# A streaming-encoder block on one core: two thirds of the depthwise taps moved from VectorE to ScalarE and GpSimd, and a fifth pair by seven products in four column groups

## The chip, the core and the metric

The kernel runs on one core of one Trainium2 chip. The metric is the device time of one execution in microseconds. Before the change it is 2029.14 us, the median of three runs (2028.86 to 2029.4). The profile is of one more execution, which took 2028.23 us.

In the profile PE is TensorE's matmuls, PEld its weight loads, DVE is VectorE, ACT is ScalarE, POOL is GpSimd and SP is SyncE, whose queue issues most DMAs.

## The reference

One layer over 256 rows of width 4096, all in float32. The part that the change touches is the first half: a norm, a wide input product, attention on 16 heads of 128, and beside it a convolution module whose depthwise part has 31 taps over 2048 channels.

```python
xn = rms_norm(h, norm_in_g[i])
proj = xn @ w_in[i]                       # 4096 x 14336
q, k, v, z_a, a_c, g_c, z_c = jnp.split(proj, ...)
y_a = chunked_attention(q, k, v, rel_table[i])
...
u = a * jax.nn.sigmoid(g)                 # conv_module
u = jnp.pad(u, ((0, 0), (CONV_K - 1, 0), (0, 0)))
u = depthwise(u, w_dw) + b_dw             # 31 causal taps for each of 2048 channels
u = jax.nn.silu(layer_norm(u, ln_g, ln_b))
y_c = u @ w_pw + b_pw
...
h = h + jnp.concatenate([y_a, y_c], axis=-1) @ w_out[i]
gate = jax.nn.sigmoid(rms_norm(h, ple_norm_g[i]) @ w_ple_gate[i] + b_ple_gate[i])
h = h + gate * (p[i] @ w_ple[i])
```

## The kernel before

**Products.** Every large product is made in float32 precision from parts that TensorE takes at its fast rate. A weight tile `wt` (128 x 1024: two column groups of 512) comes by DMA; ScalarE casts its high part `wh` (L204) and VectorE subtracts to get the low part `wl` (L205, `parts_of`). Each block product is then three matmuls of 128 x 512: high by high, low by high, high by low. Three tiles each of `wh` and `wl` rotate, and five of `wt`.

**Pairs by seven products.** `mixed_product` (L342) makes two column groups at once. It goes over 16 pairs of 128-row blocks, in an order that a text table gives. A plain pair takes eight block products, 24 matmuls. A pair marked `*` or `+` takes seven, 21 matmuls (Strassen's way): VectorE adds up the needed sums of weight blocks (`ua`, `ub`, L467 to L475) and each of the two sum tiles is cast and subtracted in turn (`uh`, `ul`). For a `+` the first sums come from the DMA: SP's queue loads a tile and GpSimd's queue adds a second transfer on top of it (L421), issued up to three pairs ahead by `sums_ahead`. The sums on the side of the activations (`combinations`) are made once and kept.

**Stages.** `scaled_pair` (L524) makes one such product from the input weights and scales it on the way out; its last four instructions on VectorE are L538. The program calls it in this order: convolution group 0, convolution group 1, (q0, k0), (v0, v1), attention 0, convolution group 2, (q1, k1), attention 1, convolution group 3, (q2, k2), (q3, v2), attention 2, layer norm, (k3, v3). The groups use the tables `early` (four pairs by seven), `early_five` (five) or `early_six` (six).

**Taps.** After a convolution group, `glu_conv` (L736) transposes the gated result to channels by time (`uT`, four blocks of 128 channels by 256) and puts 4 x 31 small jobs into the list `later`. Each is one instruction on VectorE, `conv_tap` (L718): `cv = uT * tap + cv` over 226 to 256 elements, both tensors in SBUF. `fill(n)` takes the next n jobs from `later`; `mixed_product` calls it after each pair with a number from a table (`early_fills`, `six_fills`), so the taps of one group run among the weight subtractions of the next ones:

```python
early_fills = (5, 6, 1, 5, 6, 1, 5, 6, 1, 5, 6, 1, 2, 5, 5, 4)
for i in range(4):
    for k in reversed(range(TAPS)):
        later.append(partial(conv_tap, cv, uT, i, 4 * c + i, k))
```

Each engine runs its instructions in the order of the program as the scheduler wrote it, so an instruction that waits holds up everything behind it on its engine. GpSimd before the change has little to do: the accumulating DMAs (L421), four memsets of the attention bias (L943) and a handful of tiny powers (L139).

Of the kernel before, what the change touches and what calls it, by code (L numbers as in the profile page):

```python
# [25 lines left out]
def hybrid_block(  # L26
# [23 lines left out]
    nc = tc.nc  # L50
    _, T, D = x.shape
# [5 lines left out]
    TAPS = w_dw.shape[1]  # L57
    PAD = TAPS - 1
# [23 lines left out]
    spool = pool("spool", 2, first_scratch, 1)  # L82
# [11 lines left out]
    o_q, o_k, o_v, o_za = 0, AW, 2 * AW, 3 * AW  # L94
# [117 lines left out]
    recent = []  # L212

    @contextmanager
    def queued_behind(made):

        with ExitStack() as queued:
            for ins in made:
                queued.enter_context(tc.issue_after(ins.ins))
            yield  # L220
# [112 lines left out]
    early_six = units("1 3 5 0+ 7 2* 9 4+ 11 6* 13 8+ 15 10* 12 14")  # L333

    early_fills = (5, 6, 1, 5, 6, 1, 5, 6, 1, 5, 6, 1, 2, 5, 5, 4)
    six_fills = (6, 6, 1, 5, 1, 5, 1, 5, 1, 5, 1, 5, 1, 6, 7, 7)
    norm = units("1 3 5 7 9 11 0+ 13 2* 15 4+ 8 6* 10 12 14")
    norm_fills = (7, 8, 8, 8, 6, 4, 2, 3, 2, 3, 2, 2, 0, 6, 5, 5)
# [379 lines left out]
    def conv_tap(cv, uT, i, b, k):  # L718
# [4 lines left out]
        else:  # L723
# [2 lines left out]
                cv[:, i, PAD - k :], ALU.mult, ALU.add,  # L726
            )

    def more_combinations(pair):

        if pair in (7, 9):
            c = (pair + 1) // 2
            xS[2 * c] = act.tile([P, 2, 2, T], F32R, tag="act", name="comb_x"), 0
            later.extendleft(reversed(combinations(c)))

    def glu_conv(c):  # L736
        if c == 0:
            sg, gate = scaled_pair(
                w_in0, o_a, o_g - o_a, first, r_x, (1,), begin=first_pairs
            )  # L740
        else:
            sg, gate = scaled_pair(
                w_in0, o_a + c * NB, o_g - o_a,
                *((early, r_x, early_fills) if c == 1 else (early_six, r_x, six_fills)),
                ahead=more_combinations if c == 2 else None,
            )
        for h in range(NH):
            nc.scalar.activation(gate[:, h, :], gate[:, h, :], AF.Sigmoid)
            tt(sg[:, h, :], sg[:, h, :], gate[:, h, :], ALU.mult)
        uT = spool.tile([P, 4, T], F32, tag="hd", name="uT", bufs=5)  # L750
        for pair in range(2):
            pt = tmp_psum()
            for i in range(2):
                for h in range(NH):
                    b = 2 * pair + i
                    nc.tensor.transpose(
                        pt[:, i * T + h * P : i * T + (h + 1) * P],
                        sg[:, h, b * P : (b + 1) * P],
                        ident,
                    )  # L760
            nc.scalar.copy(
                uT[:, 2 * pair : 2 * pair + 2, :], pt.rearrange("q (i t) -> q i t", t=T)
            )
        cv = act.tile([P, 4, T], F32, tag="act", name="cv")
        for i in range(4):
            for k in reversed(range(TAPS)):
                later.append(partial(conv_tap, cv, uT, i, 4 * c + i, k))
        conv.append(cv)


# [116 lines left out]
    def attention(g):  # L887
        qT, kT, v, bias = qs[g], ks.pop(g), vs.pop(g), biases.pop(g)
        y = qT.rearrange("q g (h d) -> q h g d", h=NH)
        for hd in range(GH):  # L890
            sp = tmp_psum()
            nc.tensor.matmul(sp[:, :P], qT[:, hd, :P], kT[:, hd, :P], start=True, stop=True)  # L892
            nc.tensor.matmul(sp[:, P : P + T], qT[:, hd, P:], kT[:, hd, :], start=True, stop=True)  # L893
            s = spool.tile([P, P + T], F32, tag="s", name="s")
            nm = spool.tile([P, NH], F32, tag="nm", name="nm")
            den = spool.tile([P, NH], F32, tag="den", name="den")
            for h, (lo, hi) in enumerate(((0, P), (P, P + T))):
                n = hi - lo
                nc.vector.scalar_tensor_tensor(
                    s[:, lo:hi], sp[:, lo:hi], HD ** -0.5, bias[:, hd, n - 1 :: -1],  # L900
                    ALU.mult, ALU.add,
                )
                nc.vector.tensor_reduce(nm[:, h : h + 1], s[:, lo:hi], AX.X, ALU.max, negate=True)
                nc.scalar.activation(
                    s[:, lo:hi], s[:, lo:hi], AF.Exp, bias=nm[:, h : h + 1],
                    accum_out=den[:, h : h + 1],
                )
            nc.vector.reciprocal(den, den)
            pt = tmp_psum()
            for j in range(3):  # L910
                nc.tensor.transpose(pt[:, j * P : (j + 1) * P], s[:, j * P : (j + 1) * P], ident)  # L911
            pT = spool.tile([P, 3 * P], F32, tag="pT", name="pT")
            nc.scalar.copy(pT, pt[:, : 3 * P])
            o = tmp_psum()
            vc = slice(hd * HD, (hd + 1) * HD)
            nc.tensor.matmul(o[:, :HD], pT[:, :P], v[:, 0, vc], start=True, stop=True)  # L916
            nc.tensor.matmul(o[:, HD : 2 * HD], pT[:, P : 2 * P], v[:, 0, vc], start=True, stop=False)
            nc.tensor.matmul(o[:, HD : 2 * HD], pT[:, 2 * P :], v[:, 1, vc], start=False, stop=True)
            for h in range(NH):
                nc.scalar.activation(  # L920
                    y[:, h, hd], o[:, h * HD : (h + 1) * HD], AF.Identity, scale=den[:, h : h + 1]
                )
        for h in range(NH):
            square_sum(ssq_a[:, h, g : g + 1], y[:, h])
        y_a.append(y)
# [29 lines left out]
    def heads(*parts, order=None, fills=early_fills, **kw):  # L955

        cols = [o + g * NB for o, g in parts]
        tiles = scaled_pair(
            w_in0, cols[0], cols[1] - cols[0], order or early, r_x, fills,
            homes=[home if o == o_v else dict(tag="stage") for o, _ in parts], **kw  # L960
        )
        for (o, g), t in zip(parts, tiles):
            if o == o_v:
                vs[g] = t
            else:
                (queries_of if o == o_q else keys_of)(g, t)
# [6 lines left out]

    n_g = H // GH
    assert n_g == CW // NB == 4
    glu_conv(0)
    glu_conv(1)
    load_bias(0)
    heads((o_q, 0), (o_k, 0))
    heads((o_v, 0), (o_v, 1))  # L980
    attention(0)
    glu_conv(2)
    load_bias(1)
    heads((o_q, 1), (o_k, 1))
    attention(1)
    glu_conv(3)
    load_bias(2)
    heads((o_q, 2), (o_k, 2))
    heads((o_q, 3), (o_v, 2), order=early_five)
    attention(2)  # L990
    layer_norm_swish()
# [270 lines left out]
    def weigh(h, j):  # L1262
        pin(tt(z[h][j], hs[c0 + j][:, h, :], fgs[j], ALU.mult))
# [88 lines left out]
```

## Time and profile before

| | |
|---|---|
| median of three runs | 2029.14 us |
| profiled execution | 2028.23 us |
| its span, first to last instruction | 2026.5 us |
| mean granted TensorE clock | 0.998 |
| PE busy | 2010.8 us, 9073 matmuls |
| DVE busy | 1903.4 us |
| ACT busy | 1215.0 us |
| POOL busy | 46.9 us |
| taps on VectorE (L724) | 480, 203.6 us busy |
| accumulating DMAs from GpSimd's queue (L421) | 31 |

A stretch of the windows view gives the busy time of each engine between two moments; comparing PE with DVE in one stretch says which of the two is near its limit there. The mean time of an instruction is from its start to its end; on VectorE and ScalarE the next one may start a little before that end, so the busy time of a group of neighbours is less than count times mean.

### The profile page before, as it was taken

How to read it: one execution, taken by the hardware profiler on the slowest of the kernel's cores; microseconds unless marked ns; L12 is line 12 of the kernel's file. 1: busy time of each engine (PE TensorE's matmuls, PEld its weight loads, DVE VectorE, ACT ScalarE, POOL GpSimd, SP SyncE). 2: the span in 40 equal slices, each digit the busy share in tenths (PEclk: the TensorE clock that was granted, in tenths of full speed). 3: DMA queues.
4: the chain of work that ended last, by engine and by line, in shares of the span. 5: the costliest groups of instructions: out<-in, count | busy, mean ns of one | idle time of the engine just before them, and what ended most of it. 6: DMA issues, size and time to landing. Idle time of an engine off the chain costs nothing.

```text
span 2026.5 us, 26195 instructions
## 1 busy us (share of the span) xinstructions
PE 2010.8 (99%) x9073; PEld 1654.4 (82%) x9073; DVE 1903.4 (94%) x2708; ACT 1215.0 (60%) x1583; POOL 46.9 (2%) x50
## 2 busy tenths in 40 slices
PE   9999999999999999999999999999999999999997
PEld 7888888888888888788888888888888888888876
DVE  7999999889999997888899999999999999999998
ACT  7655545655655555776556556666665666655555
POOL 0000000000000000000000000000000000000000
PEclk9999999999999999999999999999999999999999
DMA  8787878678678867456666666676666656666765
GB/s 295 222 238 234 255 217 250 177 247 240 188 221 246 252 198 241 156 177 209 196 208 207 208 204 211 208 239 210 203 211 197 208 194 201 208 218 207 231 207 180
DMA packets 171168, 436.70 MB, mean 215 GB/s; under 512 B 13966, under 2 KB 17182, under 8 KB 171034
## 3 DMA queue, kind: packets, MB, share of 16 engines
q1 hardware_dynamic: 161952, 417.93, 63.9%
q0 software_dynamic: 8432, 16.25, 4.8%
q8 instruction: 71, 1.16, 0.2%
q10 hardware_dynamic: 650, 0.84, 0.1%
q14 instruction: 63, 0.52, 0.1%
HBM read 430.77 MB, written 4.19 MB: 215 GB/s over the span
## 4 chain that ended last, share of the span: by engine, by line
PE 95%; DVE 3%; issue 1%; ACT 1%; DMA 0%; POOLq 0%; POOL 0%; ACTq 0%; SPq 0%; DVEq 0%
PE acc L385 73%; PE acc_P L385 17%; PE tmp_ps L170 1%; DVE cv L724 1%; PE acc L229 1%; DVE wl L205 1%; PE tmp_ps L893 0%; PE tmp_ps L877 0%; PE tmp_ps L911 0%; PE tmp_ps L916 0%; PE acc L373 0%; ACT wh L204 0%; PE tmp_ps L892 0%; DVE ul L205 0%; DMA xin<-in_x_dram 0%
## 5 line engine op out<-in xcount | busy, mean ns | idle before, releaser
L385 PE MATMUL acc<-wh,big_t 128*128 128x512 f32 x4154 | 1283.3, 391 | 0.6 <-DVE y_c L1043 0.4
L204 ACT CAST wh<-wt 128x1024 fp32r<-128x1024 f32 (+1 forms) x737 | 710.1, 974 | 523.3 <-PE acc L385 364.3
L385 PEld LDWEIGHTS acc<-wh,big_t 128*128 128x128 f32 x4154 | 777.0, 188 | 160.8 <-DVE y_c L1043 0.9
L205 DVE TENSOR_TENSOR wl<-wt,wh 128x1024 fp32r<-128x1024 f32 (+1 forms) x737 | 817.4, 1122 | 39.9 <-ACT wh L204 33.6
L385 PE MATMUL acc<-wl,big_t 128*128 128x512 f32 x2077 | 801.9, 391 | 0.1
L385 PEld LDWEIGHTS acc<-wl,big_t 128*128 128x128 f32 x2077 | 389.5, 188 | 82.5 <-DVE wl L205 1.8
L204 ACT CAST uh<-ua 128x1024 fp32r<-128x1024 f32 x174 | 182.9, 1052 | 91.1 <-DVE ua L468 46.3
L205 DVE TENSOR_TENSOR ul<-ua,uh 128x1024 fp32r<-128x1024 f32 x174 | 212.0, 1219 | 9.6 <-ACT uh L204 8.1
L724 DVE SCALAR_TENSOR_TENSOR cv<-uT,dw,cv 128x250 f32<-128x250 f32 (+19 forms) x480 | 203.6, 464 | 1.1
L385 PE MATMUL acc_P<-uh,big_t 128*128 128x512 f32 x528 | 161.8, 392 | 0.0
L204 ACT CAST uh<-ub 128x1024 fp32r<-128x1024 f32 x92 | 96.8, 1052 | 95.5 <-DVE ub L475 79.2
L205 DVE TENSOR_TENSOR ul<-ub,uh 128x1024 fp32r<-128x1024 f32 x92 | 112.2, 1220 | 6.7 <-ACT uh L204 5.6
L385 PEld LDWEIGHTS acc_P<-uh,big_t 128*128 128x128 f32 x528 | 98.0, 188 | 23.2 <-ACT uh L204 3.7
L385 PE MATMUL acc_P<-ul,big_t 128*128 128x512 f32 x264 | 101.3, 392 | 0.0
L467 DVE TENSOR_TENSOR ua<-wt 128x512 f32<-128x512 f32 x102 | 69.9, 685 | 17.3 <-DMA wt<-in_w_in_dram 10.7
L385 PE MATMUL acc<-uh,big_t 128*128 128x512 f32 x266 | 82.5, 390 | 0.0
L385 PE MATMUL acc_P<-wh,big_t 128*128 128x512 f32 x266 | 82.1, 389 | 0.0
L468 DVE TENSOR_TENSOR ua<-wt 128x512 f32<-128x512 f32 x102 | 69.6, 683 | 4.3 <-DMA wt<-in_w_in_dram 3.6
L385 PE MATMUL acc_P<-uh,comb_t 128*128 128x512 f32 x228 | 70.1, 390 | 0.1
L475 DVE TENSOR_TENSOR ub<-ub,wt 128x512 f32<-128x512 f32 x92 | 63.0, 685 | 0.8
L474 DVE TENSOR_TENSOR ub<-ua,wt 128x512 f32<-128x512 f32 x92 | 62.9, 683 | 0.3
L385 PEld LDWEIGHTS acc_P<-ul,big_t 128*128 128x128 f32 x264 | 49.3, 188 | 12.5 <-DVE ul L205 2.0
(243 smaller groups left out, 1485.5 us busy)
## 6 DMA issues: line engine op xcount, KB each, us to landing
wt<-in_w_in_dram SPq DMA_DIRECT2D x416, 512.0 KB, 4.5
wt<-in_w_out_dram SPq DMA_DIRECT2D x128, 512.0 KB, 4.3
wt<-in_w_ple_gate_dram SPq DMA_DIRECT2D x128, 512.0 KB, 4.2
wt<-in_w_pw_dram SPq DMA_DIRECT2D x32, 512.0 KB, 4.8
ua<-in_w_in_dram SPq DMA_DIRECT2D x31, 512.0 KB, 4.3
ua<-in_w_in_dram POOLq DMA_DIRECT2D x31, 512.0 KB, 8.7
wt<-in_w_in_dram SPq DMA_DIRECT2D x31, 256.0 KB, 2.8
hc<-in_x_dram SPq DMA_DIRECT2D x8, 512.0 KB, 4.7
```

The lines of the kernel that those rows point to most:

```text
L170: nc.tensor.transpose(pt[:, i * T + h * P : i * T + (h + 1) * P], src[:, h, b] if len(src.shape) == 4 else src[:, h, b * P : (b + 1) * P], ...
L204: nc.scalar.copy(wh[:, :kc, :], wt[:, :kc, :]),
L205: nc.vector.tensor_tensor(wl[:, :kc, :], wt[:, :kc, :], wh[:, :kc, :].bitcast(F32), ALU.subtract),
L229: nc.tensor.matmul(acc, a, b[:, k, :], start=kb == 0 and kind == 0, stop=kb == kblocks - 1 and kind == 2,)
L385: nc.tensor.matmul(banks[name], a, b, start=name not in begun, stop=final and ends[name] == n and kind == 2 and not (left and name in "P2 ...
L467: plus(ua[:, 0], w0[:, 0], w0[:, 1])
L468: plus(ua[:, 1], w0[:, 1], w1[:, 1])
L474: plus(ub[:, 0], ua[:, 0], w1[:, 1])
L475: plus(ub[:, 1], ub[:, 0], w1[:, 0])
L724: nc.vector.scalar_tensor_tensor(cv[:, i, PAD - k :], uT[:, i, : T + k - PAD], dw[:, b, k : k + 1], cv[:, i, PAD - k :], ALU.mult, ALU.add,)
```

## The change

Of the 31 taps of a channel, 20 (k = 1, 2, 4, 5, 7, 8 and so on) no longer run on VectorE. For each of them and each group of four blocks, ScalarE makes four products `uT * tap` (L763 of the changed kernel, 227 to 255 elements each) into a product tile `wu`, and GpSimd adds that tile to a second tile of its own (L767, four blocks at once). The first tap after a new pair of tiles is written by ScalarE straight into the sum tile, whose head GpSimd sets to zero. When the tiles change or a group ends, VectorE adds the sum tile to `cv` once (`gather`, 128 x 1024). There is one product tile and one sum tile at a time; `weighted_in` says in which pool they lie. The other 11 taps stay on VectorE. The product instructions are queued on ScalarE behind the latest weight cast (`queued_behind(recent[:1])`).

The groups (q0, k0), (v0, v1), (q1, k1) and (q2, k2) change from `early` to `early_five`, with the new table `five_fills`. The combinations for the activation side that the fifth pair needs are made in convolution group 1 rather than 2.

```diff
+    five_fills = (5, 7, 6, 2, 6, 5, 2, 5, 2, 5, 2, 5, 1, 2, 2, 2)
...
+    def weighted_in(*homes):
+
+        while halves:
+            fill(1)
+        gather()
+        weighted[:] = homes
+
+    def gather():
+
+        if gathered:
+            cv, total = gathered
+            gathered.clear()
+            tt(cv, cv, total, ALU.add)
+
+    def weigh(cv, uT, b, k, blocks):
+
+        n, first = T + k - PAD, not gathered
+        if blocks[0] == 0:
+            if not hasattr(weighted[0], "rearrange"):
+                weighted[:] = [spool.tile([P, 4, T], F32, name="wu", **kw) for kw in weighted]
+            halves.append(k)
+            opening[:] = [first]
+            if first:
+                gathered[:] = [cv, weighted[1]]
+                nc.gpsimd.memset(weighted[1][:, :, : PAD - k], 0.0)
+        else:
+            halves.clear()
+        total = weighted[1][:, :, PAD - k :]
+        to = total if opening[0] else weighted[0][:, :, :n]
+        with queued_behind(recent[:1]):
+            for i in blocks:
+                nc.scalar.activation(
+                    to[:, i], uT[:, i, :n], AF.Identity, scale=dw[:, b + i, k : k + 1]
+                )
+        if blocks[0] and not opening[0]:
+            nc.gpsimd.tensor_tensor(total, total, to, ALU.add)
...
-                ahead=more_combinations if c == 2 else None,
+                ahead=more_combinations if c == 1 else None,
...
-        for i in range(4):
-            for k in reversed(range(TAPS)):
-                later.append(partial(conv_tap, cv, uT, i, 4 * c + i, k))
+        def taps(k, blocks):
+            later.extend(partial(conv_tap, cv, uT, i, 4 * c + i, k) for i in blocks)
+
+        taps(PAD, range(4))
+        for k in range(0, PAD, 3):
+            for n in range(2):
+                for blocks in ((0, 1), (2, 3)):
+                    later.append(partial(weigh, cv, uT, 4 * c, k + 1 + n, blocks))
+                    taps(k, (2 * n + blocks[0] // 2,))
+        later.append(gather)
...
     glu_conv(0)
+    weighted_in(home, home)
     glu_conv(1)
     load_bias(0)
-    heads((o_q, 0), (o_k, 0))
-    heads((o_v, 0), (o_v, 1))
+    weighted_in(home, home)
+    heads((o_q, 0), (o_k, 0), **five)
+    weighted_in(stage, stage)
+    heads((o_v, 0), (o_v, 1), **five)
```

On GpSimd before, from the first norm on (`ua` is a tile of weight sums, `bias` the attention bias, `r_x` the norm's scale), there is nothing but DMA issues and a memset:

```order
L139 TENSOR_TENSOR r_x<-r_x,mhalf 128x2
L421 DMA ua<-in_w_in_dram 128x2x512 x6
L943 MEMSET bias 64x4x64
L421 DMA ua<-in_w_in_dram 128x2x512 x11
L943 MEMSET bias 64x4x64
L421 DMA ua<-in_w_in_dram 128x2x512 x7
```

On GpSimd after the change, at the same place, in convolution group 1 (`wu` is the product tile and also the sum tile):

```order
L422 DMA ua<-in_w_in_dram 128x2x512 x2
L756 MEMSET wu 128x4x29
L767 TENSOR_TENSOR wu<-wu 128x4x228
L767 TENSOR_TENSOR wu<-wu 128x4x230
L422 DMA ua<-in_w_in_dram 128x2x512
L767 TENSOR_TENSOR wu<-wu 128x4x231
L767 TENSOR_TENSOR wu<-wu 128x4x233
L767 TENSOR_TENSOR wu<-wu 128x4x234
L422 DMA ua<-in_w_in_dram 128x2x512
L767 TENSOR_TENSOR wu<-wu 128x4x236
```

Two or three adds of four blocks each now stand between one accumulating DMA and the next.

On VectorE before, early in convolution group 1, a tap stands between any two pieces of weight work:

```order
L205 TENSOR_TENSOR wl<-wt,wh 128x1024
L724 SCALAR_TENSOR_TENSOR cv<-uT,dw,cv 128x250
L205 TENSOR_TENSOR ul<-ua,uh 128x1024
L724 SCALAR_TENSOR_TENSOR cv<-uT,dw,cv 128x249
L205 TENSOR_TENSOR wl<-wt,wh 128x512
L724 SCALAR_TENSOR_TENSOR cv<-uT,dw,cv 128x248
L474 TENSOR_TENSOR ua<-ua,wt 128x512
L724 SCALAR_TENSOR_TENSOR cv<-uT,dw,cv 128x247
L475 TENSOR_TENSOR ua<-ua,wt 128x512
```

On VectorE after, from the first taps of the same group on:

```order
L721 TENSOR_SCALAR cv<-uT,dw,prm 128x256 x4
L725 SCALAR_TENSOR_TENSOR cv<-uT,dw,cv 128x226 x4
L725 SCALAR_TENSOR_TENSOR cv<-uT,dw,cv 128x229 x2
L205 TENSOR_TENSOR wl<-wt,wh 128x1024 x2
L205 TENSOR_TENSOR ul<-ua,uh 128x1024
L205 TENSOR_TENSOR wl<-wt,wh 128x512
L475 TENSOR_TENSOR ua<-ua,wt 128x512
L291 TENSOR_TENSOR comb<-big_t 128x512
L476 TENSOR_TENSOR ua<-ua,wt 128x512
L268 TENSOR_TENSOR comb<-comb 128x128
```

The weight work stands almost without taps between, and the combinations (L268, L291) are now here.

On ScalarE after, later in convolution group 1 (`wh` and `uh` are the high parts), where before there were casts alone:

```order
L204 CAST wh<-wt 128x1024
L763 ACTIVATE wu<-uT,dw 128x236 x4
L204 CAST wh<-wt 128x1024
L204 CAST uh<-ua 128x1024
L204 CAST wh<-wt 128x512
L204 CAST wh<-wt 128x1024
L204 CAST uh<-ua 128x1024
L763 ACTIVATE wu<-uT,dw 128x237 x4
L204 CAST wh<-wt 128x1024 x2
L763 ACTIVATE wu<-uT,dw 128x239 x4
```

Four products stand between casts, and the next four may begin only when GpSimd has added the ones before.

More of the change, by code (lines that the diff above doesn't have):

```diff
@@ L727, in conv_tap @@
             )
+    weighted, gathered, halves = [], [], []
+    def weighted_in(*homes):
[29 more added lines that the diff above has]
+            nc.gpsimd.tensor_tensor(total, total, to, ALU.add)
+    opening = []
     def more_combinations(pair):
@@ L975, in hybrid_block @@
     assert n_g == CW // NB == 4
+    stage, five = dict(tag="stage"), dict(order=early_five, fills=five_fills)
     glu_conv(0)
+    weighted_in(home, home)
     glu_conv(1)
     load_bias(0)
-    heads((o_q, 0), (o_k, 0))
-    heads((o_v, 0), (o_v, 1))
+    weighted_in(home, home)
+    heads((o_q, 0), (o_k, 0), **five)
+    weighted_in(stage, stage)
+    heads((o_v, 0), (o_v, 1), **five)
     attention(0)
+    weighted_in(home, home)
     glu_conv(2)
     load_bias(1)
-    heads((o_q, 1), (o_k, 1))
+    weighted_in(home, home)
+    heads((o_q, 1), (o_k, 1), **five)
     attention(1)
+    weighted_in(home, home)
     glu_conv(3)
     load_bias(2)
-    heads((o_q, 2), (o_k, 2))
+    weighted_in(home, home)
+    heads((o_q, 2), (o_k, 2), **five)
+    weighted_in(stage, home)
     heads((o_q, 3), (o_v, 2), order=early_five)
```

## The prediction

> **What bounds the kernel now.** The page comes first, then the chain of work that ended last, then stages cut at the ends of the input products.
>
> ```profile
> span 2026.5 us, 26195 instructions
> PE 2010.8 (99%) x9073; PEld 1654.4 (82%) x9073; DVE 1903.4 (94%) x2708; ACT 1215.0 (60%) x1583; POOL 46.9 (2%) x50
> PE 95%; DVE 3%; issue 1%; ACT 1%; DMA 0%; POOLq 0%; POOL 0%; ACTq 0%; SPq 0%; DVEq 0%
> ```
>
> TensorE sets the time and VectorE stands close behind it. The next view gives the busy time of every engine in nine stages; each stage ends with the fourth L538 of one `scaled_pair` (columns: stretch, its length, then PE, PEld, DVE, ACT, POOL with their instruction counts).
>
> ```profile
> 98.60:183.80 85.20, 85.03 (x379) 70.05 (x378) 85.18 (x141) 44.40 (x49) 6.07 (x5) 1.00 0.85 247
> 183.80:269.20 85.40, 85.40 (x382) 70.72 (x381) 85.40 (x141) 44.22 (x49) 5.18 (x5) 1.00 0.82 240
> 269.20:355.60 86.40, 86.40 (x391) 71.69 (x390) 86.05 (x144) 45.22 (x51) 4.87 (x4) 1.00 0.79 232
> 355.60:445.60 90.00, 90.00 (x418) 74.06 (x417) 73.40 (x101) 55.23 (x82) 3.65 (x3) 1.00 0.70 212
> 445.60:531.30 85.70, 85.65 (x382) 70.66 (x381) 85.65 (x141) 45.60 (x50) 5.17 (x5) 1.00 0.83 241
> 531.30:623.40 92.10, 92.10 (x435) 76.07 (x435) 85.03 (x134) 57.45 (x86) 3.66 (x3) 1.00 0.69 207
> 623.40:709.20 85.80, 85.78 (x382) 70.72 (x381) 85.75 (x142) 45.60 (x50) 5.18 (x5) 1.00 0.82 240
> 709.20:794.40 85.20, 85.20 (x386) 70.75 (x384) 80.02 (x112) 45.77 (x51) 3.95 (x4) 1.00 0.77 231
> sum 791.70, PE 790.84 PEld 652.01 DVE 749.59 ACT 455.03 POOL 39.36; mean PE 87.87 PEld 72.45 DVE 83.29 ACT 50.56 POOL 4.37
> ```
>
> Call them S1 to S8 in this order. In S1, S2, S3, S5 and S7 VectorE has no idle time left, yet TensorE loses only 791.70 - 790.84 = 0.86 us in all nine stages of the view. So VectorE is just at its limit: less work there gives almost nothing by itself, and more work gives a stall at once. The same view of the taps alone (L724, DVE) shows where they stand:
>
> ```profile
> 98.60:183.80 85.20, 32.92 (x78) 1.00 0.85 247
> 183.80:269.20 85.40, 32.86 (x80) 1.00 0.82 240
> 269.20:355.60 86.40, 31.94 (x72) 1.00 0.79 232
> 445.60:531.30 85.70, 32.73 (x78) 1.00 0.83 241
> 531.30:623.40 92.10, 18.09 (x42) 1.00 0.69 207
> 623.40:709.20 85.80, 32.81 (x78) 1.00 0.82 240
> 709.20:794.40 85.20, 17.74 (x42) 1.00 0.77 231
> ```
>
> **What TensorE gains.** From the timeline of TensorE in S1:
>
> ```profile
> 150.04 0.62 PE L385 MATMUL acc<-wh,big_t 128*128 128x512 f32 x2
> 150.49 0.39 PE L385 MATMUL acc<-wl,big_t 128*128 128x512 f32 x1
> 150.72 0.62 PE L385 MATMUL acc<-wh,big_t 128*128 128x512 f32 x2
> ```
>
> Three matmuls take 150.72 - 150.04 = 0.68 us. A plain pair has 24, a pair by seven products 21. Four groups (S2, S3, S5, S7) get one more such pair each: 4 x 0.68 = **2.7 us less**.
>
> **What VectorE loses and gains.** Durations of one instruction, from the groups by line and form (mean ns behind the busy time) and, last, from the rows on the tile cv:
>
> ```profile
> L205 DVE TENSOR_TENSOR wl<-wt,wh 128x1024 fp32r<-128x1024 f32 x604 | 729.2, 1218 | 39.6 <-ACT wh L204 33.3 <-ACT qT L920 2.3 <-PE tmp_ps L170 1.5
> L205 DVE TENSOR_TENSOR ul<-ua,uh 128x1024 fp32r<-128x1024 f32 x174 | 212.0, 1219 | 9.6 <-ACT uh L204 8.1 <-PE acc L385 1.2
> L205 DVE TENSOR_TENSOR wl<-wt,wh 128x512 fp32r<-128x512 f32 x133 | 90.8, 683 | 0.4 <-ACT wh L204 0.3
> L475 DVE TENSOR_TENSOR ua<-ua,wt 128x512 f32<-128x512 f32 x41 | 28.2, 687 | 0.3
> L798 DVE TENSOR_TENSOR lnsum<-lnsum,cv x2: 1215/1216/1216, 784.8 to 787.0; 128x1024 f32<-128x1024 f32 x2
> ```
>
> One group's step from four to five sevens adds two ul (2.44), one half wl (0.68) and six sums (4.1), and takes away one wl (1.22): +6.0 us. A gather is a 128x1024 sum like L798: 1.2 us. A tap costs 32.92 / 78 = 0.42 us. By the new order S1 to S3 keep 30, 27 and 23 taps, S5 31, S6 9, S7 31, S8 9.
>
> - S1 to S3: 256.6 us of VectorE, less 150 x 0.42 = 63.7, plus two sevens 12.0, plus four gathers 4.9: 209.8. The combinations that move from S3 to S1 stay inside this sum.
> - S5: 85.65 - 47 x 0.42 + 6.0 + 1.2 = 73.1. S7: the same, 73.1.
> - S6: 85.0 - 33 x 0.43 + 1.2 = 72. S8: 80.0 - 14.0 + 1.2 = 67.
>
> **What GpSimd's adds cost.** There are 72, by the order 13, 12, 11, 0, 13, 5, 13, 5 in S1 to S8, of some 4 x 242 = 968 elements. No such add is in the trace; the nearest rows:
>
> ```profile
> masks.py:199 POOL TENSOR_SCALAR_AFFINE_SELECT ident<-ident 128x128 f32<-128x128 f32 x1 | 0.3, 288 | 0.0
> L132 POOL MEMSET mean_w<- 128x128 f32 x1 | 0.2, 204 | 0.0
> L134 POOL MEMSET mhalf<- 128x2 f32 x1 | 0.1, 96 | 0.0
> ```
>
> Writing takes (204 - 96) / 126 = 0.86 ns an element above 0.1 us; reading once and writing, 1.52, so a read adds 0.66. From below, an add runs at the pace of the write alone: 0.94 us. From above, at two whole read-and-write passes: 3.0 us. I take one write and two reads, 2.18 ns an element: **2.2 us**, an estimate nearest to the affine select, the only row that reads and writes. The Trainium skill (GPSIMD Engine Reference, 3.1 Elementwise — side-by-side cycle accounting) has 4497 ns for 2048 elements, an estimate of 2.13 us here, and by it the sum below would be 4 us less; this trace has no such add to compare.
>
> Does an add hold VectorE up? GpSimd's few powers of two elements tell something. First the timeline around one of them (start, length), where VectorE is busy, then around another, where VectorE stands still as it starts:
>
> ```profile
> 834.69 1.22 DVE L205 TENSOR_TENSOR ul<-ua,uh 128x1024 fp32r<-128x1024 f32 x1
> 834.86 1.63 POOL L139 TENSOR_TENSOR r_ln<-r_ln,mhalf 128x2 f32<-128x2 f32 x1 [48.84 <-DVE r_ln L138]
> ```
>
> ```profile
> 990.03 0.69 POOL L139 TENSOR_TENSOR r_c<-r_c,mhalf 128x2 f32<-128x2 f32 x1 [72.09 <-DVE r_c L138]
> ...
> 990.27 0.69 DVE L467 TENSOR_TENSOR ua<-wt 128x512 f32<-128x512 f32 x1 [0.32 <-DMA wt<-in_w_in_dram]
> ```
>
> The power takes 0.69 us in the quiet place and 1.63 us where VectorE is inside a subtraction of two SBUF tiles: it ends 0.58 us after that subtraction's end (834.69 + 1.22 = 835.91), as if its reading had waited for it. I read this as one path to SBUF that both engines read by, which one of them holds while the other waits. Nearly all VectorE work of these stages (L205, the sums, the taps) reads two SBUF tiles. That the wait goes the other way too, behind a long add, is my step beyond the rows. A gain is excluded: an add gives VectorE nothing that it lacks today.
>
> The second place bounds the hold from below: L467, two SBUF tiles too, began 0.24 us into the power and took its usual 0.69, so the path is free again once GpSimd has read. For an add of 968 elements the reading is at least 968 x 2 x 0.66 = 1.28 us and at most the whole add. I take the whole, since a sum needs its last elements only at its end. The Trainium skill (SBUF — State Buffer, Who interferes with whom) says that whichever of the two issues second is fully blocked until the first has finished its whole instruction. The trace agrees for the power behind the subtraction (1.63 us) and differs for L467 behind the power (0.69, not held). By that rule the time would be 2093; by the row's shortest hold, 2036.
>
> **The sum.** A stage lasts as long as the longer of TensorE and VectorE plus adds.
> - S1 to S3: 209.8 + 36 x 2.2 = 289.0, against 257.0 before: +32.0.
> - S5: 73.1 + 13 x 2.2 = 101.7 against 85.7: +16.0. S7: +15.9.
> - S6: 72 + 11 = 83 under TensorE's 92.1; S8: 78 under 85.2: nothing. S4 has no add.
>
> Together +63.9; where VectorE sets the stage, the 2.7 us of TensorE bring nothing. The span 2026.5 becomes 2090.4. The profiled execution took 2028.23, 1.7 more than its span, and the median 2029.14 lies 0.9 above that: **2093**.
>
> Left at nothing are ScalarE's 320 products and what else the change queues up; the nearest rows for these, from the groups by form, the waits and the DMA issues:
>
> ```profile
> L156 ACT ACTIVATE big_t<-tmp_ps,prm 128x256 fp32r<-128x256 f32 x64 | 27.7, 470 | 4.1 <-DVE big_t L157 2.5 <-PE tmp_ps L170 1.6
> ACT wh L204 <- PE acc L385: 364.3, 279, 3.5
> ua<-in_w_in_dram SPq DMA_DIRECT2D x31, 512.0 KB, 4.3
> ua<-in_w_in_dram POOLq DMA_DIRECT2D x31, 512.0 KB, 8.7
> ```
>
> At 0.47 us, 56 of them put 26 us into S5, with 45.6 + 1.7 of casts 73 of 85.7: covered by the 364 us in which ScalarE now waits for free buffers. Where it isn't covered: the product tile is single, so a product waits for the add before it, and the weight casts queued behind that product wait too, then L205, then TensorE. VectorE's eight gathers wait for the last add of a tile, with L205 subtractions queued behind them; the add itself is in the sum already, its four products (1.9 us) are not: at worst 8 x 1.9 = 15. So a miss here is upward. GpSimd's queue also issues 27 accumulating DMAs between adds. They go out three pairs ahead, 3 x 24 x 0.227 = 16.3 us, and need 4.3 + 8.7 = 13.0; one add in front (2.2) fits, a second would make ScalarE's uh wait, 1 us at a time. SP loads fewer sums (27 for 31) and waits for none of this.
>
> **Rivals.**
> - *The add holds VectorE only while it reads* (1.28 us): S1 to S3 255.9, S5 and S7 89.7; +6.8 in all, **2036**. For it: the L467 row. Against: a long add reads throughout.
> - *ScalarE is the new wait, with no shared path.* Each add of 2.2 us less one cast of 1.05 in front of the next product stalls ScalarE 1.15 x 13 = 15 us in a stage: 73 + 15 = 88, 3 over, five stages: **2044**. For it: the single tile. Against: three buffers of wh and wl lie between a cast and its matmul.
> - *The change does what it says: the adds cost VectorE nothing.* Then VectorE falls to 73 of 85 and TensorE sets every stage: 2029.14 - 2.7 = **2026.4**, not slower. It decides where an add holds VectorE for less than (85.0 - 73.1) / 13 = 0.9 us. For it: the L467 row again. Against: the 1.63 us. More than 0.2% would need 4.1 us, and 2.7 + 0.86 of TensorE's idle is less.
>
> **How the numbers follow.** Whole hold 0.66, reading only 0.07, ScalarE 0.06, no cost 0.21. The likeliest gives 2093. Its own ends come from the add: near 0.94 us nothing is left of it; 3.0 us gives S1 to S3 317.8, S5 and S7 112.1, +113 or 2143. The range runs from the no-cost case, 2025, to 2140 and leaves out little more than the top. A measurement of this kernel can tell about 0.2%, 4 us, from no change: slower 0.79 (the first three cases), same 0.15, faster 0.06 (the last case, with TensorE gaps that the busy time hides).
>
> **What would show it.** Right: VectorE's two-input rows that follow an add lengthen or start late by about 2 us, S1, S2, S3, S5 and S7 grow by 5 to 16 us, TensorE idles behind L205, S4 keeps its 90 us. Reading only: the same with half the size. ScalarE: idle before products or casts, put down to GpSimd's adds, and VectorE with gaps. No cost: every stage at TensorE's length, four of them 0.7 us shorter. Wrong altogether: adds far from 2.2 us.

## The result, and the profile after

The changed kernel takes **2122.07 us** (median of 4 runs, 2120.04 to 2122.9) against 2029.0 (2028.83 to 2029.4) for the kernel before on the same chip: a ratio of **1.0458**, 95% interval 1.0446 to 1.047. It is 93 us slower; 64 were forecast. In one of e4's ten executions below TensorE ran at a mean granted clock of 0.757 and the kernel took 2495.45 us; that one moves e4's median by 0.1 us and is counted in no ratio or range. From the page of the changed kernel:

```profile
span 2121.1 us, 26354 instructions
PE 2042.7 (96%) x9061; PEld 1654.3 (78%) x9061; DVE 1933.9 (91%) x2428; ACT 1339.6 (63%) x1911; POOL 230.9 (11%) x126
PE 73%; DVE 13%; issue 6%; ACT 4%; POOL 2%; DMA 1%; ACTq 0%; POOLq 0%; DVEq 0%; SPq 0%
L205 DVE TENSOR_TENSOR wl<-wt,wh 128x1024 fp32r<-128x1024 f32 (+1 forms) x737 | 857.9, 1180 | 69.5 <-ACT wh L204 62.4
L767 POOL TENSOR_TENSOR wu<-wu 128x912 f32<-128x912 f32 (+11 forms) x72 | 189.5, 2632 | 308.6 <-ACT wu L763 305.8
L763 ACT ACTIVATE wu<-uT,dw 128x227 f32<-128x227 f32 (+19 forms) x320 | 135.8, 488 | 74.1 <-POOL wu L767 72.6
L725 DVE SCALAR_TENSOR_TENSOR cv<-uT,dw,cv 128x226 f32<-128x226 f32 (+9 forms) x160 | 102.5, 690 | 0.0
```

Read the third line first: TensorE's share of the chain fell from 95% to 73%, and VectorE, ScalarE and GpSimd came in. Then the durations. VectorE has 280 instructions fewer than before (2428 for 2708) and is busy for longer (1933.9 for 1903.4). The same two groups on the page of the kernel before:

```profile
L205 DVE TENSOR_TENSOR wl<-wt,wh 128x1024 fp32r<-128x1024 f32 (+1 forms) x737 | 817.4, 1122 | 39.9 <-ACT wh L204 33.6
L724 DVE SCALAR_TENSOR_TENSOR cv<-uT,dw,cv 128x250 f32<-128x250 f32 (+19 forms) x480 | 203.6, 464 | 1.1
```

A tap now lasts 690 ns in the mean instead of 464, and the subtraction L205 1180 instead of 1122: the same work, stretched. The stages, cut as in the prediction (eight of the nine; the sum has the ninth too):

```profile
98.90:199.40 100.50, 90.54 (x383) 70.94 (x381) 92.13 (x106) 67.02 (x108) 35.60 (x20) 0.98 0.73 207
199.40:304.00 104.60, 93.08 (x377) 71.66 (x377) 92.92 (x100) 66.24 (x107) 39.68 (x17) 0.95 0.63 189
304.00:400.90 96.90, 88.14 (x380) 69.13 (x381) 90.20 (x89) 63.54 (x99) 31.91 (x15) 1.00 0.65 198
400.90:491.50 90.60, 90.60 (x420) 74.54 (x419) 69.86 (x92) 55.14 (x82) 3.86 (x4) 1.00 0.69 212
491.50:596.20 104.70, 90.88 (x383) 69.26 (x381) 96.03 (x103) 68.59 (x109) 39.61 (x18) 1.00 0.63 191
596.20:693.60 97.40, 94.21 (x430) 76.35 (x431) 81.78 (x102) 65.45 (x109) 15.86 (x9) 0.98 0.64 195
693.60:798.40 104.80, 91.83 (x383) 70.60 (x381) 96.13 (x104) 68.62 (x109) 39.51 (x18) 0.98 0.63 190
798.40:887.60 89.20, 87.02 (x381) 71.36 (x382) 77.84 (x81) 53.42 (x74) 15.56 (x9) 0.98 0.73 220
sum 884.50, PE 821.48 PEld 651.00 DVE 779.89 ACT 579.53 POOL 223.23; mean PE 91.28 PEld 72.33 DVE 86.65 ACT 64.39 POOL 24.80
```

The sum grew by 884.5 - 791.7 = 92.8 us, which is nearly the whole loss. S4, the one stage without adds, kept its length (90.6 for 90.0). In the stages that lost most, no engine is busy from end to end any more: S5 lasts 104.7, with TensorE busy for 90.9 and VectorE for 96.0.

To see what stretched VectorE, I compared each of its instructions with the shortest of the same line and shape, and summed what was over it by more than 0.15 us (call it **held time**). In the stages, beside the number of adds and the growth of the stage:

| stage | adds | VectorE instructions held | held, us | stage grew by, us | forecast, us |
|---|---|---|---|---|---|
| S1 | 13 | 12 | 19.6 | 15.3 | |
| S2 | 12 | 11 | 18.0 | 19.2 | S1 to S3: 32.0 |
| S3 | 11 | 11 | 19.9 | 10.5 | |
| S4 | 0 | 0 | 0 | 0.6 | 0 |
| S5 | 13 | 12 | 20.5 | 19.0 | 16.0 |
| S6 | 5 | 4 | 7.4 | 5.3 | 0 |
| S7 | 13 | 12 | 20.5 | 19.0 | 15.9 |
| S8 | 5 | 5 | 8.4 | 4.0 | 0 |

Nearly every add holds one VectorE instruction, and none is held elsewhere: 67 instructions, 114.3 us. All 67 end as if they had begun their work at the add's end: the time from there to their own end is 0.11 to 0.25 us less than their usual length. Two stretches of the timeline of VectorE and GpSimd (start, length, engine and line) show one hold each:

```profile
159.55 1.87 POOL L767 TENSOR_TENSOR wu<-wu 128x948 f32<-128x948 f32 x1 [9.54 <-ACT wu L763]
160.37 3.26 DVE L205 TENSOR_TENSOR wl<-wt,wh 128x1024 fp32r<-128x1024 f32 x2 [1.26 <-ACT wh L204]
```

```profile
184.98 0.69 DVE L516 TENSOR_TENSOR z<-acc_P,z 128x512 f32<-128x512 f32 x1
185.11 2.65 POOL L767 TENSOR_TENSOR wu<-wu 128x972 f32<-128x972 f32 x1
185.70 0.69 DVE L517 TENSOR_TENSOR z<-acc_P,z 128x512 f32<-128x512 f32 x1
186.68 2.18 DVE L205 TENSOR_TENSOR wl<-wt,wh 128x1024 fp32r<-128x1024 f32 x1 [0.28 <-ACT wh L204]
```

In the first, an add ends at 159.55 + 1.87 = 161.42. The second row merges two L205 of 1024 elements each, which usually take 1.21 us and overlap by 0.08, 2.34 us together; here they take 3.26. The first starts inside the add, takes 2.12 us and ends 1.1 us after the add, about its own length. In the second, L516 and L517 take one operand from PSUM and run at their usual 0.69 us beside the add; L205, with two SBUF operands, started 1.08 us before the add's end (187.76) and took 2.18 instead of 1.22. So a held instruction, with both operands in SBUF, does its work after the add, not beside it.

### The profile page after: what moved, and what is told of

It is laid out like the page before. It is cut to its first block, busy times and chain, and to the rows that moved or that the text cites. A ratio compares the mean times of both kernels' runs of the same rounds, so it can differ in the third digit from the quotient of the medians.

```text
span 2121.1 us, 26354 instructions
## 1 busy us (share of the span) xinstructions
PE 2042.7 (96%) x9061; PEld 1654.3 (78%) x9061; DVE 1933.9 (91%) x2428; ACT 1339.6 (63%) x1911; POOL 230.9 (11%) x126
## 3 DMA queue, kind: packets, MB, share of 16 engines
q8 instruction: 71, 1.16, 0.2%
## 4 chain that ended last, share of the span: by engine, by line
PE 73%; DVE 13%; issue 6%; ACT 4%; POOL 2%; DMA 1%; ACTq 0%; POOLq 0%; DVEq 0%; SPq 0%
PE acc L386 55%; PE acc_P L386 14%; DVE wl L205 6%; POOL wu L767 2%; DVE ul L205 2%; ACT wu L763 2%; ACT wh L204 1%; DVE cv L725 1%; PE tmp_ps L170 1%; DVE ua L475 1%; PE acc L229 1%; DVE ua L476 1%; ACT uh L204 0%; PE tmp_ps L926 0%; PE tmp_ps L942 0%
## 5 line engine op out<-in xcount | busy, mean ns | idle before, releaser
L386 PE MATMUL acc<-wh,big_t 128*128 128x512 f32 x4098 | 1270.3, 392 | 3.4 <-DVE z L539 1.6
L205 DVE TENSOR_TENSOR wl<-wt,wh 128x1024 fp32r<-128x1024 f32 (+1 forms) x737 | 857.9, 1180 | 69.5 <-ACT wh L204 62.4
L386 PEld LDWEIGHTS acc<-wh,big_t 128*128 128x128 f32 x4098 | 769.1, 189 | 162.4 <-ACT wh L204 3.8
L204 ACT CAST uh<-ua 128x1024 fp32r<-128x1024 f32 x182 | 191.2, 1051 | 160.4 <-DVE ua L476 97.3
L205 DVE TENSOR_TENSOR ul<-ua,uh 128x1024 fp32r<-128x1024 f32 x182 | 229.5, 1261 | 18.5 <-ACT uh L204 18.2
L767 POOL TENSOR_TENSOR wu<-wu 128x912 f32<-128x912 f32 (+11 forms) x72 | 189.5, 2632 | 308.6 <-ACT wu L763 305.8
L763 ACT ACTIVATE wu<-uT,dw 128x227 f32<-128x227 f32 (+19 forms) x320 | 135.8, 488 | 74.1 <-POOL wu L767 72.6
L205 DVE TENSOR_TENSOR ul<-ub,uh 128x1024 fp32r<-128x1024 f32 x92 | 112.2, 1220 | 6.3 <-ACT uh L204 5.7
L386 PEld LDWEIGHTS acc_P<-uh,big_t 128*128 128x128 f32 x528 | 98.0, 188 | 23.9 <-ACT uh L204 4.4
L725 DVE SCALAR_TENSOR_TENSOR cv<-uT,dw,cv 128x226 f32<-128x226 f32 (+9 forms) x160 | 102.5, 690 | 0.0
L468 DVE TENSOR_TENSOR ua<-wt 128x512 f32<-128x512 f32 x110 | 77.0, 700 | 22.2 <-DMA wt<-in_w_in_dram 15.4
L469 DVE TENSOR_TENSOR ua<-wt 128x512 f32<-128x512 f32 x110 | 82.7, 752 | 5.3 <-DMA wt<-in_w_in_dram 5.0
```

Source lines behind the costliest of these rows:

```text
L204: nc.scalar.copy(wh[:, :kc, :], wt[:, :kc, :]),
L205: nc.vector.tensor_tensor(wl[:, :kc, :], wt[:, :kc, :], wh[:, :kc, :].bitcast(F32), ALU.subtract),
L386: nc.tensor.matmul(banks[name], a, b, start=name not in begun, stop=final and ends[name] == n and kind == 2 and not (left and name in "P2 ...
L468: plus(ua[:, 0], w0[:, 0], w0[:, 1])
L469: plus(ua[:, 1], w0[:, 1], w1[:, 1])
L725: nc.vector.scalar_tensor_tensor(cv[:, i, PAD - k :], uT[:, i, : T + k - PAD], dw[:, b, k : k + 1], cv[:, i, PAD - k :], ALU.mult, ALU.add,)
```

## The experiments

The ratios below are to the kernel before on the same chip, with a 95% interval. "Cost" is the time above e1's 2032.8 us, the kernel with the same queues and no reading on GpSimd (the kernel before differed by at most 0.8 us between the chips used). Lines of dots mark what is left out of a diff.

### Reading or waiting: e1_write_only

```diff
-            nc.gpsimd.tensor_tensor(total, total, to, ALU.add)
+            for _ in range(2):
+                nc.gpsimd.memset(to, 0.0)
```

> GpSimd's add is replaced by two memsets of the product tile (the sum of the 20 taps is left out), so ScalarE still waits for GpSimd and GpSimd still works, at the pace of its memsets some 2 x 0.9 us, but reads nothing. Theory (an add holds VectorE's two-input instructions because both read by one path): no VectorE instruction of a normal 0.4 to 1.2 us lasts 2 us any more, and the time falls from 2122 to 2026 to 2035. Rival (ScalarE's waiting for GpSimd is the main loss): VectorE's rows may be normal, but the time stays above 2044, with ScalarE idle behind GpSimd as in the changed kernel, 73 us. Rival (any GpSimd instruction holds VectorE): long VectorE rows as before, time near 2122.

2032.81 us (2032.12 to 2034.05), ratio 1.0018 (1.0008 to 1.0027). GpSimd is still busy for almost 2 us behind each four products, ScalarE still waits for it, and 89 of the 93 us are gone, as the theory had it. The groups on these lines, and the taps on the tile cv (minimum, median, maximum in ns):

```profile
L768 POOL MEMSET wu<- 128x912 f32 (+14 forms) x144 | 137.2, 953 | 253.1 <-ACT wu L763 238.2
L763 ACT ACTIVATE wu<-uT,dw 128x227 f32<-128x227 f32 (+19 forms) x320 | 135.3, 489 | 23.0 <-POOL wu L768 22.1
L725 DVE SCALAR_TENSOR_TENSOR cv<-uT,dw,cv x160: 445/462/482, 106.8 to 694.3; 128x226 f32<-128x226 f32 x16, 128x229 f32<-128x229 f32 x16, 128x232 f32<-128x232 f32 x16, 128x235 f32<-128x235 f32 x16
```

The slowest tap takes 482 ns; in the changed kernel it takes 2592, from the same view:

```profile
L725 DVE SCALAR_TENSOR_TENSOR cv<-uT,dw,cv x160: 441/458/2592, 106.1 to 808.2; 128x226 f32<-128x226 f32 x16, 128x229 f32<-128x229 f32 x16, 128x232 f32<-128x232 f32 x16, 128x235 f32<-128x235 f32 x16
```

Writing alone holds no instruction of VectorE: beside these 144 memsets none is over its shortest by 0.15 us. What costs the time is that GpSimd *reads* SBUF; e10 below, whose copies last about as long as one of these memsets but read, holds VectorE again. ScalarE as the new bound, without a shared path, is out: its casts and products are queued as before, it waits 22.1 us for GpSimd, and all of that costs at most 4 us.

### The same adds on VectorE: e6_vector_adds and e9_vector_adds_four

```diff
-            nc.gpsimd.tensor_tensor(total, total, to, ALU.add)
+            nc.vector.tensor_tensor(total, total, to, ALU.add)
```

> The changed kernel with VectorE doing the 72 adds (four blocks at once, 968 elements, some 1.1 us by the 1024-element rows) instead of GpSimd. VectorE keeps 320 x 0.42 - 72 x 1.1 = 55 us of relief, without a hold. Theory: VectorE stays under TensorE in every stage, and the 2.7 us of the four sevens show: 2025 to 2029. Rival (ScalarE's order costs, as the write-only run's 3.8 us above the kernel before suggest): products that wait for VectorE's adds delay the casts, 2031 to 2040.

2034.52 (2033.91 to 2035.62), ratio 1.0024 (1.0015 to 1.0034); the theory's 2025 to 2029 is missed, and the rival's range holds it, though not for the rival's reason, as e9 shows. In e9 the groups go back to four sevens as well:

```diff
-    stage, five = dict(tag="stage"), dict(order=early_five, fills=five_fills)
+    stage, five = dict(tag="stage"), {}
```

> The run with VectorE's adds, and four pairs by seven in the four groups as before: only the way of the taps differs from the kernel before. VectorE has 55 us less to do, ScalarE 136 us more, GpSimd only its memsets. Theory (VectorE's load was no loss before, and the 5.5 us that the run with five lost came from the fifth pair's sums beside the adds): 2028 to 2031, the same as before. Rival (the products in ScalarE's queue cost by themselves): 2032 to 2036.

2030.32 (2028.81 to 2032.24), ratio 1.0004 (0.9996 to 1.0013): no difference. So 320 products on ScalarE and 72 long adds cost nothing, as long as the adds run on VectorE, where one takes 1.16 us, and most of e6's 4.8 us come with the fifth pair by seven, the one thing that e9 takes back. VectorE's busy time fell from 1903.4 to 1872.1 us by it, and that bought nothing either. This is the nearest to a version that gains, and it doesn't.

### Each part of the change alone: e4_sevens_only and e5_taps_only

e4 is the kernel before with five sevens in the four groups and the combinations moved, its taps left on VectorE:

```diff
-                ahead=more_combinations if c == 2 else None,
+                ahead=more_combinations if c == 1 else None,
...
-    heads((o_q, 0), (o_k, 0))
-    heads((o_v, 0), (o_v, 1))
+    heads((o_q, 0), (o_k, 0), order=early_five)
+    heads((o_v, 0), (o_v, 1), order=early_five)
...
-    heads((o_q, 1), (o_k, 1))
+    heads((o_q, 1), (o_k, 1), order=early_five)
...
-    heads((o_q, 2), (o_k, 2))
+    heads((o_q, 2), (o_k, 2), order=early_five)
```

> The kernel before with a fifth pair by seven in the four groups and the combinations in convolution group 1; all taps stay on VectorE, nothing goes to GpSimd. By the ledger VectorE is full, so 6 us more a group: S1 to S3 268.6 against 255.6, S5 and S7 91.6 against 85.0, 25 us more, about 2053: then the change needed relief on VectorE. Rival (VectorE's busy time hides slack, since neighbours overlap by some 0.08 us): 2026 to 2032, and the relief bought nothing.

2033.56 (2032.77 to 2034.91), ratio 1.0023 (1.0013 to 1.0033). The ledger, the prediction's sum of VectorE's work stage by stage, gave 2053 and is far off: it had taken VectorE in these stages to be full to the last. Taps slid into S4 (52 for 10) and S6 (56 for 42), which grew by about 2 us each, S2 and S3 shrank by 1.2 together, and the 24 us of added work cost 4.5. In the profiled executions 2.2 us of the difference come only after the ninth stage, where the two kernels do the same; why isn't known. So a VectorE busy for 85.40 of 85.40 us didn't mean that nothing more fitted. It also shows that the sevens bring the whole time none of the 2.7 us that they save TensorE.

e5 is the changed kernel with the line shown at e9, so its adds stay on GpSimd:

> The changed kernel with four pairs by seven in the four groups, as before; products and adds as changed. Theory (a held VectorE costs nearly its whole hold, whatever slack the stage has on paper): the adds are the same 72, so the time stays at 2105 to 2125. Rival (the stage ledger: VectorE's total decides, with its slack used up first): 24 us of weight sums less, S1 to S3 197.8 + 36 x 1.85 = 264.4, S5 and S7 91.1, some 20 us above the kernel before, 2050 to 2075.

2121.2 (2120.13 to 2122.96), ratio 1.0452 (1.0438 to 1.0466). VectorE has some 24 us less to do than in the changed kernel and not one us comes of it. Its S5:

```profile
494.70:597.20 102.50, 90.97 (x386) 71.71 (x384) 91.65 (x96) 68.49 (x111) 40.49 (x20) 0.98 0.70 200
```

VectorE stands idle for 102.5 - 91.65 = 10.9 us of a stage that is 17 us too long. A stage isn't the longer of TensorE and VectorE plus adds.

### How the cost goes with the hold: e3_half_add, e8_forty_adds, e10_copy

e3 adds two of the four blocks. e8 leaves out the adds with k % 3 = 1, which keeps 40 of 72. In e10 a copy of the products onto themselves stands in the add's place: it reads one operand, not two.

```diff
-            nc.gpsimd.tensor_tensor(total, total, to, ALU.add)
+            nc.gpsimd.tensor_tensor(total[:, :2], total[:, :2], to[:, :2], ALU.add)
```

```diff
-        if blocks[0] and not opening[0]:
+        if blocks[0] and not opening[0] and k % 3 == 2:
```

```diff
-            nc.gpsimd.tensor_tensor(total, total, to, ALU.add)
+            nc.gpsimd.tensor_copy(to, to)
```

> GpSimd adds only two of the four blocks of each product tile (the other half of the sum is left out); ScalarE's products are as they were. An undisturbed add takes 1.85 us in the changed kernel, so about 0.95 here. By the prediction's ledger an add decides from 0.9 us on: S1 to S3 209.8 + 36 x 0.95 = 244 under TensorE's 255.6, S5 and S7 73.1 + 12.4 = 85.5 against 85.0. Theory: 2026 to 2050, the lower end by the ledger, the upper if waits in a row cost as much beside the hold as in the changed kernel (half of 29 and the half clock). Rival (the number of adds counts, not their length): above 2080.

> Only 40 of the 72 adds, at full length (the other product tiles are made and never added: that part of the sum is left out). 40 x 1.85 = 74 us of GpSimd reading, as in the run with half adds (72 x 1.04 = 75 us, 2077). Theory (the time that VectorE is held counts): 2065 to 2085. Rival (the number counts, each add costing a hand-over): 2033 + 40/72 x 44 = 2057 or less. Rival (long holds cost more than in proportion, since short ones are covered by the buffers): above 2090.

> GpSimd copies the product tile onto itself instead of adding it (the sum is left out): one read and one write an element, 1.5 us by the affine select's 1.52 ns. Theory (any GpSimd instruction that reads SBUF holds VectorE's two-input instructions for its length): the runs with adds cost 55 us for each us of length above 0.2 us (1.04 us: 44, 1.85 us: 89), so 1.5 us gives some 70 above the write-only run, 2090 to 2110, or less if the copy is quicker. Rival (only an instruction with two inputs holds VectorE): 2030 to 2036.

e3: 2077.32 (2076.63 to 2081.53), ratio 1.0239 (1.0224 to 1.0255); neither range holds it. e8: 2083.98 (2081.86 to 2087.24), ratio 1.0269 (1.0255 to 1.0283), as the theory had it. e10: 2056.24 (2055.25 to 2057.06), ratio 1.0134 (1.0119 to 1.015): the rival, by which one operand holds nothing, falls, and the theory's size was too large. That the copy is quicker than expected is only part of it: by the theory's own rule 0.96 us would have cost 42, and 23.4 were measured. The instructions on GpSimd, of the changed kernel, of e3, of e8 and of e10 (minimum, median, maximum in ns):

```profile
L767 POOL TENSOR_TENSOR wu<-wu x72: 1815/2472/5321, 107.5 to 831.4; 128x912 f32<-128x912 f32 x4, 128x920 f32<-128x920 f32 x4, 128x924 f32<-128x924 f32 x4, 128x932 f32<-128x932 f32 x4
```

```profile
L767 POOL TENSOR_TENSOR wu<-wu x72: 1042/1416/4879, 107.8 to 784.1; 128x456 f32<-128x456 f32 x4, 128x460 f32<-128x460 f32 x4, 128x462 f32<-128x462 f32 x4, 128x466 f32<-128x466 f32 x4
```

```profile
L767 POOL TENSOR_TENSOR wu<-wu x40: 1852/2358/4833, 107.2 to 791.9; 128x912 f32<-128x912 f32 x4, 128x924 f32<-128x924 f32 x4, 128x936 f32<-128x936 f32 x4, 128x948 f32<-128x948 f32 x4
```

```profile
L767 POOL COPY wu<-wu x72: 957/1286/4326, 106.7 to 763.7; 128x912 f32<-128x912 f32 x4, 128x920 f32<-128x920 f32 x4, 128x924 f32<-128x924 f32 x4, 128x932 f32<-128x932 f32 x4
```

The minimum is the length that nothing disturbs; the median is longer, because GpSimd waits for VectorE just as VectorE waits for it. Held time and cost side by side:

| kernel | held, us | instructions held | cost, us |
|---|---|---|---|
| e1, no reading | 0 | 0 | 0 |
| e10, copies | 37.0 | 55 | 23.4 |
| e3, half adds | 39.6 | 46 | 44.5 |
| e8, forty adds | 63.1 | 35 | 51.2 |
| e2, two product tiles | 109.4 | 65 | 77.7 |
| e5, four sevens | 109.2 | 67 | 88.4 |
| e7, even fills | 112.4 | 67 | 88.0 |
| changed kernel | 114.3 | 67 | 89.3 |

The cost follows held time, at 0.6 to 1.1 us for each us held, and no threshold shows: half an add costs half of what an add does. Why a held us costs more in e3 than in e10 isn't settled. One difference is in their waits: in e3 VectorE stands idle for 18.5 us before its eight gathers, for the last add of a tile; in e10, whose copies don't touch the sum tile, no gather waits for GpSimd.

### ScalarE behind one product tile: e2_two_products

```diff
+                weighted.append(spool.tile([P, 4, T], F32, tag="wu2", name="wu", bufs=1))
...
-        to = total if opening[0] else weighted[0][:, :, :n]
+        to = total if opening[0] else weighted[0 if k % 3 == 1 else 2][:, :, :n]
```

The room comes from the two buffers of pT, of which it keeps one.

> A second product tile, so that ScalarE's next products no longer wait for the add of the ones before; the adds are as they were (attention's transposed tile has one buffer instead of two, to make room). Theory, in which the hold costs some 64 us by the ledger and ScalarE's waiting makes up part of the remaining 29: the time falls by 10 to 30, to 2092 to 2112, ScalarE's 73 us behind GpSimd mostly go, and VectorE's long rows stay. Rival (the hold and TensorE's half clock alone make the 93): ScalarE's waits go and the time stays within 5 us of 2122. Rival (ScalarE's wait is the main loss): below 2060.

2110.48 (2108.51 to 2112.37), ratio 1.0398 (1.0383 to 1.0414). The product's wait for the add fell from 72.6 us to 13.9, held time hardly changed (109.4), and 11.6 us came back. That is the price of the single tile.

### Bunched or spread: e7_even_fills

```diff
-    five_fills = (5, 7, 6, 2, 6, 5, 2, 5, 2, 5, 2, 5, 1, 2, 2, 2)
+    five_fills = (4, 4, 4, 3, 4, 4, 4, 3, 4, 4, 4, 3, 4, 4, 3, 3)
```

> The changed kernel with 3 or 4 jobs after every pair of the four groups instead of 1 to 7. Theory (the loss arises pair by pair: where two or three adds fall on one pair, VectorE is held longer than the three buffers of weight parts cover): spreading the adds lowers the time by 10 to 40, to 2080 to 2112. Rival (each add costs its hold wherever it stands): within 8 us of 2122. Rival (the table had put the adds beside plain pairs, where VectorE has room, and evening puts them beside the sevens): above 2130.

2120.82 (2117.94 to 2124.81), ratio 1.0444 (1.0428 to 1.046). Spreading taps and products evenly over a group changes nothing: an add costs its hold wherever it stands.

## Why the prediction was right and wrong, step by step

**Right: the direction, the mechanism and the places.** The add holds VectorE up, the price is its reading (e1), and S1 to S3, S5 and S7 lose most while S4 doesn't. The step that went "beyond the rows", from a power that waits for VectorE to a VectorE that waits for an add, holds. The rule of the Trainium skill (SBUF — State Buffer, Who interferes with whom), that the second is blocked until the first has finished, fits the 67 held instructions, L205 at 186.68 among them: all get their work done only after the add's end. Which of the two comes second can't be told from the starts in the trace, though (last section). The rival by which an add holds only while it reads put the reading at 1.28 us, so it would have let VectorE go about half a microsecond before the end of an undisturbed add; it fell, and L467 beside the tiny power told nothing about long adds. Its price of a read, 0.66 ns an element, isn't borne out either: a copy takes 0.96 us where a memset of the tile takes 0.86 (the shortest of e10 and e1).

**Wrong: the length of an add.** 2.2 us were taken; undisturbed, one of 920 to 948 elements takes 1.82 to 1.87 us. It was oversized, and an add met VectorE after it had run for a while: the hold is 114.3 / 72 = 1.6 us per add, against 2.2. By this alone the loss would have been smaller than forecast: with 1.6 in the prediction's sum S1 to S3 come to 267.4 and S5 and S7 to 93.9, some 27 us in all. That 64 lies as near to 93 as it does is luck, since the oversized add made up for part of the next error.

**Wrong, and the step that failed: "a stage lasts as long as the longer of TensorE and VectorE plus adds".** It let VectorE's free time take up 72 x 2.2 = 158 us of holds down to 64. In the run 93 us are lost against 114 held. S6 and S8 were to lose nothing and lost 9.3; S5 had 104.7 - 96.0 = 8.7 us of idle VectorE and lost 19.0 all the same. e5 shows it best: 24 us less work on VectorE, no gain. And there is no point at 0.9 us per add below which a hold costs nothing, which the no-cost rival was built on: e3 and e10, with 0.55 and 0.51 us held per add, still lose 44.5 and 23.4.

What takes its place, as far as the rows show it, is a chain through queues that run in order. One hold, followed on four engines of the changed kernel (start, length; in brackets the idle time before and what ended it):

```profile
532.10 2.65 POOL L767 TENSOR_TENSOR wu<-wu 128x944 f32<-128x944 f32 x1 [1.82 <-ACT wu L763]
532.59 2.70 DVE L475 TENSOR_TENSOR ua<-ua,wt 128x512 f32<-128x512 f32 x1
...
536.20 1.21 DVE L205 TENSOR_TENSOR wl<-wt,wh 128x1024 fp32r<-128x1024 f32 x1
536.31 1.04 ACT L204 CAST uh<-ua 128x1024 fp32r<-128x1024 f32 x1 [3.43 <-DVE ua L476]
...
537.47 0.50 PE L386 MATMUL acc<-wl,big_t 128*128 128x512 f32 x1 [2.41 <-DVE wl L205]
```

The add holds L475, a weight sum of 0.68 us, for 2.02 us. The second half of the sum (L476) comes late behind it, and ScalarE, whose next cast needs it, stands for 3.43 us with its later casts and products queued up; L205 stands behind the sum too, and TensorE waits 2.41 us for its result. By the time VectorE is free again the loss has been passed on to TensorE, and less work on VectorE later doesn't bring it back. In the waits of the whole kernel (total us, times, longest), each of these links is there:

```profile
ACT wh L204 <- PE acc L386: 237.8, 203, 3.6
ACT uh L204 <- DVE ua L476: 97.3, 38, 5.3
ACT wu L763 <- POOL wu L767: 72.6, 47, 4.1
PEld acc L386 <- DVE wl L205: 63.8, 61, 3.2
DVE wl L205 <- ACT wh L204: 62.4, 83, 1.9
PE acc L386 <- DVE wl L205: 39.9, 39, 2.8
```

and without GpSimd's reading, in e1, those of TensorE for L205 are all but gone and ScalarE's for the sum is 38.5 us instead of 97.3, while VectorE's for the casts is no smaller, so that one isn't shown to come from the holds:

```profile
ACT wh L204 <- PE acc L386: 264.0, 226, 3.5
ACT uh L204 <- DVE ua L476: 38.5, 22, 3.8
DVE wl L205 <- ACT wh L204: 86.0, 97, 4.8
PEld acc L386 <- DVE wl L205: 2.8, 6, 1.0
PE acc L386 <- DVE wl L205: 0.5, 1, 0.5
```

That the chain, and not another property of the stage, keeps VectorE from making up for a hold is argued from these rows. A fourth buffer of weight parts would test it; no run has one.

**Wrong: what was left at nothing.** ScalarE behind the single product tile costs 11.6 us (e2); its wait in front of products was named as an upward miss and not priced. The gathers' wait for the adds, named at 15 us at worst, comes to 7.8 us in the trace. The accumulating DMAs, which a second add in front was to make late, did no harm: no wait of ScalarE for them is in the trace. TensorE's clock was not thought of at all (below).

**Right in direction, too firm in size: "VectorE is just at its limit".** e4's 24 us more cost 4.5, e9's 31 us less nothing. Its full busy time before hid work that could be done later.

## What to carry to other kernels

Before moving elementwise work to GpSimd, count what it reads: here each long add or copy lengthened the VectorE instruction that it met, nearly always one with two SBUF operands, until its own end, and most of that reached the kernel's time, although VectorE had free time. A balance of busy times per stage says nothing about a short stall in a chain of queues that run in order; price a hold at its full length first, and take slack off only where a run shows it. And where an engine's busy time is 100%, test with a small load whether it is full or only early.

## What had not been expected of the hardware

**TensorE at half its clock.** Before, the granted clock stays at full speed through these stages. In the changed kernel it drops to half in six stretches of 3.4 to 6.8 us, 23.9 us in all, each right after TensorE had waited. TensorE's timeline around the first one:

```profile
150.46 0.61 PE L386 MATMUL acc<-wh,big_t 128*128 128x512 f32 x2
153.38 0.50 PE L386 MATMUL acc<-wl,big_t 128*128 128x512 f32 x1 [2.30 <-DVE wl L205]
153.72 0.88 PE L386 MATMUL acc<-wh,big_t 128*128 128x512 f32 x2
154.40 0.63 PE L386 MATMUL acc<-wl,big_t 128*128 128x512 f32 x1
154.83 1.05 PE L386 MATMUL acc<-wh,big_t 128*128 128x512 f32 x2
...
157.36 0.62 PE L386 MATMUL acc_P<-wh,big_t 128*128 128x512 f32 x2
```

and the window over that stretch, with the granted clock as the third number from the end:

```profile
154.00:158.00 4.00, 4.00 (x12) 3.17 (x11) 3.97 (x7) 1.19 (x2) 0.00 (x0) 0.58 0.71 209
```

After an idle time of 2.3 us a `wl` matmul is 0.43 us ahead of the next instead of 0.23, for about 4 us; the busy time reads 4.00 of 4.00 all the while. At half rate, 23.9 us lose at most 12 of the 93. e1 and e10 have no such stretch, e3 and e8 6.8 us, e2 23.9, e5 27.3, e7 30.7. No run has the holds without the half clock at full length, so its share isn't shown by itself. The Trainium skill (TensorE: Matmul & The Clock Gate, Part 1: The HAM clock gate) tells of a clock that halves after an idle window of some 3.4 us; here shorter waits were enough: single ones of 2.2 to 2.8 us before five of the six stretches, and 1.4 and 1.6 us close together before the other. A wait of 2.41 us (at 537.47) had no such stretch behind it, so the trace gives no sharp bound.

**GpSimd doesn't get in between any two instructions of VectorE.** An add that takes 1.85 us undisturbed takes up to 5.3 us where subtractions and taps follow each other without a gap, and 2.47 in the median. In the changed kernel 24 VectorE instructions with two SBUF operands begin inside an add and run at their usual length; 23 of them end at least 1.68 us before the add does. So these adds had started in the trace and not yet got in, and what holds VectorE is the last 1.7 us or so. And a one-operand instruction of VectorE on SBUF is not safe either: the first taps' L721, 407 ns in the median, took up to 2430 in the changed kernel and no more than 413 in e1.

```profile
L721 DVE TENSOR_SCALAR cv<-uT,dw,prm x16: 400/407/2430, 104.8 to 701.4; 128x256 f32<-128x256 f32 x16
```
